# One-hot rows turned by ScalarE, value parts added in PSUM, and the sums of two layers kept by tokens

## The chip, the cores and the metric

The kernel runs on one core of a Trainium2 chip. The metric is the device time of one execution in microseconds (us), here the median of three runs. A profiled execution gives the trace that the rows below are from.

## What is computed

Two transformer blocks follow each other on 256 tokens of width 1024, all in float32. What the change touches is the second half of the first block, a layer that picks 16 experts per head out of 16384 (8 heads, so 128 picks per token), and the last layer of the second block:

```python
def peer(h, wq, subkeys, u, v):
    ...
    s1, i1 = lax.top_k(s[:, :, 0], P_TOPK)
    s2, i2 = lax.top_k(s[:, :, 1], P_TOPK)
    cand = (s1[..., :, None] + s2[..., None, :]).reshape(T, P_HEADS, P_TOPK * P_TOPK)
    sc, ci = lax.top_k(cand, P_TOPK)
    e = ...  # the first key's index * 128 + the second key's index
    g = jax.nn.softmax(sc, axis=-1)
    ...
        z = jnp.einsum('thkd,td->thk', jnp.take(u, eb, axis=0), hb)
        a = (jax.nn.gelu(z) * gb)
        return jnp.einsum('thk,thkd->td', a, jnp.take(v, eb, axis=0))

# first block:   x = x + g2 * rms_norm(peer(h), norm2_post)
# second block:  x = x + jnp.square(jax.nn.relu(h @ w_up)) @ w_down
```

## The kernel before, in words

Nothing is gathered. The kernel computes z for all 16384 experts and all tokens as dense products (128 chunks of 128 experts, `z_chunks`), applies gelu, multiplies each z by a weight that is zero for experts a token did not pick, and multiplies the result by the whole of v (128 chunks again, `out_chunks`). The order is: queries and routing beside z chunks 0 to 43, z chunks 44 to 95, output chunks 0 to 31, z chunks 96 to 127, output chunks 32 to 127. Four tiles `zt[0]` to `zt[3]` hold 32 chunks of z each.

Every product of two float32 matrices is made of three matmuls of type fp32r: each operand is split into a high part and a low part (`wh`, `wl`; `hh`, `hl`; `ah`, `al`), and high by high, low by high and high by low are added in PSUM (`mm3`, L184 to L186). For weights, `split` does this on the fly: a 1 MB block comes by DMA (`raw`), ScalarE (ACT) casts half of it to `wh` (L164), and VectorE (DVE) or GpSimd (POOL) subtracts to get `wl` (L165). Which engine subtracts is a set of half-block numbers given to `chunks` as `pool_`; for z's weights it was halves 0 to 49 and every second one up to 94. There are three buffers each of `raw`, `wh` and `wl` in this part of the program, so the weights are ready two to three chunks ahead at most. A z chunk and an output chunk are 24 matmuls each, of 128x128 weights and 256 columns. For the output, `acc_k` keeps the sums by features: the 128x128 blocks of v are loaded as weights, the 256 tokens are streamed.

The weight of an expert for a token comes from two one-hots. `weights_of(s, n)` treats n groups of 32 chunks at once, in three passes (group 0, groups 1 and 2, group 3), in blocks of TB = 16 tokens: `o1` (L1023) is, for every token, the one-hot of the first key's index, as a row of 128; `o2` (L1027) is the one-hot of the second index, with tokens innermost; `og` (L1031) is `o2` times the two parts (high, low) of the softmax value. One float16 matmul per token (L1038) has `o1`'s row block as weights and streams both parts of `og` side by side: 64 columns for n = 1, 128 for n = 2, and since tokens are innermost, one column lies 32 bytes from the next. ACT and DVE then add the two parts (L1041, L1042) and DVE multiplies z (L1046). `weights_of` is a generator: `advance(bg, n)` runs n of its steps (up to the next `yield`) after each chunk, with the rates NW, NX, NY, and `drain` runs what is left. The routing is a generator too (`bgr`, rate NR).

After the last output chunk the sums of squares go over the partitions by matmuls (`sums`, `norm`), the result is scaled and added to x (`residual`), and the parts of the next layer's input are made. The first half-blocks of the second block's first weights are split ahead, in places given by `LB`; the `wl` of all six are on POOL. In the last layer, `wup` and `wdn` chunks alternate; `acc_k` sums `wdn` by features as well.

Instructions stand on each engine's queue in one fixed order; what cannot start holds up all behind it on that queue.

Of the kernel before, what the change touches and what calls it, by code (L numbers as in the profile page):

```python
# [22 lines left out]
TB = 16  # L23
# [10 lines left out]
LB = ('qaee',(0,1,2,3,4,5))  # L34
KO = 3
F2 = (5,10)
KA = 0
KB = 2
PU = (4,50,1)
NZ, NR, NW, ZR, NX, NY = (7, 1.75, 1, 44, 0.8, 1)  # L40
# [71 lines left out]
def body(ctx: ExitStack, tc: tile.TileContext, a: dict):  # L112
# [125 lines left out]
    def acc_k(acc, *steps, first=False, last=False, order=range(8), then=lambda j: None):  # L238

        for j in order:  # L240
# [3 lines left out]
            then(j)  # L244

# [572 lines left out]
    with ExitStack() as p2:  # L818
# [197 lines left out]
        def weights_of(s, n):  # L1016


            m = 32 * n
            for b in range(S // TB):  # L1020
# [4 lines left out]
                yield  # L1025
# [3 lines left out]
                og = op_.tile([128, 2, 64, TB], F16, tag="og", name="og", bufs=2)[:, :, :m]  # L1029
# [455 lines left out]
```

## Time and profile before

| | |
|---|---|
| median of 3 runs | 1618.21 us (1616.15 to 1618.53) |
| the profiled execution | 1615.83 us |
| its span (first to last instruction) | 1614.0 us |
| TensorE (PE) matmuls busy | 1536.8 us, 95% of the span |
| VectorE (DVE) busy | 1235.1 us, 77% |
| ScalarE (ACT) busy | 762.0 us, 47% |
| GpSimd (POOL) busy | 243.6 us, 15% |
| mean granted TensorE clock | 0.972 of full speed |

The span is what the trace covers; 1.83 us of the profiled execution lie around it. Matmuls overlap each other in the pipeline, so "PE busy" says when PE had work, and not how fast it went: the pace is read from the starts of successive matmuls. The stages of the part that changes are: routing with z chunks (371 to 558 us in the trace), z with the first pass of weights (558 to 745), output and z with the second pass (745 to 970), the rest of the second pass alone (970 to 994), output with the third pass (994 to 1162), output alone (1162 to 1298), and the join to the second block (1298 to 1328). The last layer is at 1434 to 1614.

### The profile page before, as it was taken

The page shows a single profiled execution, that of the slowest core. Times are in us where ns is not written, and L with a number is a line of the kernel's source. Part 1 is how long each engine was busy: PE and PEld are TensorE (multiplying, and loading weights), DVE is VectorE, ACT ScalarE, POOL GpSimd, SP SyncE. Part 2 cuts the span into 40 slices and gives each one's busy share as a digit, 9 for nine tenths or more (in the row PEclk, how much of TensorE's full clock was granted, in tenths as well). Part 3 has the DMA queues.
Part 4 walks back from the last instruction along what each step waited for, and adds up shares of the span by engine and source line. Part 5 has one row for each costly group of instructions (what it writes and reads, how often), then busy time and mean ns, then how long its engine had stood idle before and what let it go on. Part 6 is the DMA issues. An engine that isn't in the chain of part 4 may idle for free.

```text
span 1614.0 us, 29532 instructions
## 1 busy us (share of the span) xinstructions
PE 1536.8 (95%) x12164; PEld 1475.0 (91%) x12164; DVE 1235.1 (77%) x2231; ACT 762.0 (47%) x1263; POOL 243.6 (15%) x109
## 2 busy tenths in 40 slices
PE   5899999989888999999999997999999989999998
PEld 4898899979888999999899985999999979899998
DVE  8978796677969999887877778888755578666555
ACT  3544454445435434444444443444444458754442
POOL 3300000034436843330000000000000030000000
PEclk7999999999999999999999997999999989999999
DMA  9456594534433534444434341444455535344542
GB/s 347 178 196 240 204 336 175 185 120 169 168 132 134 182 134 153 150 144 161 173 134 154 134 156 51 157 153 145 159 191 190 183 121 183 105 155 186 183 184 79
DMA packets 40025, 269.82 MB, mean 167 GB/s; under 512 B 4433, under 2 KB 5201, under 8 KB 9170
## 3 DMA queue, kind: packets, MB, share of 16 engines
q1 hardware_dynamic: 38882, 264.67, 45.5%
q10 hardware_dynamic: 1008, 3.27, 0.6%
q8 instruction: 95, 1.56, 0.4%
q14 instruction: 40, 0.33, 0.1%
HBM read 266.87 MB, written 1.05 MB: 166 GB/s over the span
## 4 chain that ended last, share of the span: by engine, by line
PE 83%; DVE 14%; ACT 2%; issue 1%; DMA 0%; SPq 0%; DVEq 0%; ACTq 0%
PE mm L184 12%; PE mm L186 12%; PE mm L185 12%; PE acc L185 10%; PE acc L186 10%; PE acc L184 10%; PE g L1038 7%; DVE wl L165 1%; DVE cand L877 1%; DVE scr L411 1%; DVE x L342 1%; DVE pr L917 1%; DVE o L1023 1%; PE mm L218 1%; DVE i L871 1%
## 5 line engine op out<-in xcount | busy, mean ns | idle before, releaser
L164 ACT CAST wh<-raw 128x1024 fp32r<-128x1024 f32 x449 | 470.0, 1049 | 623.6 <-PE mm L185 315.1
L165 DVE TENSOR_TENSOR wl<-raw,wh 128x1024 fp32r<-128x1024 f32 x361 | 441.8, 1229 | 175.8 <-ACT wh L164 173.1
L186 PE MATMUL mm<-hh,wl 128*128 128x256 f32 x1816 | 516.4, 284 | 12.3 <-DVE wl L165 12.0
L184 PE MATMUL mm<-hh,wh 128*128 128x256 f32 x1816 | 521.5, 287 | 4.4 <-ACT z L854 4.4
L185 PE MATMUL mm<-hl,wh 128*128 128x256 f32 x1816 | 513.4, 283 | 0.0
L186 PEld LDWEIGHTS mm<-hh,wl 128*128 128x128 f32 x1816 | 346.6, 191 | 15.0 <-DVE wl L165 13.7
L184 PEld LDWEIGHTS mm<-hh,wh 128*128 128x128 f32 x1816 | 345.9, 190 | 11.3 <-ACT z L854 4.6
L185 PEld LDWEIGHTS mm<-hl,wh 128*128 128x128 f32 x1816 | 346.6, 191 | 0.8 <-issue 0.2
L165 POOL TENSOR_TENSOR wl<-raw,wh 128x1024 fp32r<-128x1024 f32 x89 | 227.1, 2558 | 492.5 <-PE mm L312 252.8
L184 PE MATMUL acc<-ah,wh 128*128 128x256 f32 x1024 | 289.4, 283 | 2.0 <-ACT ah L248 2.0
L185 PE MATMUL acc<-al,wh 128*128 128x256 f32 x1024 | 288.6, 282 | 0.0
L186 PE MATMUL acc<-ah,wl 128*128 128x256 f32 x1024 | 288.4, 282 | 0.0
L184 PEld LDWEIGHTS acc<-ah,wh 128*128 128x128 f32 x1024 | 194.6, 190 | 3.9 <-ACT ah L248 2.5
L185 PEld LDWEIGHTS acc<-al,wh 128*128 128x128 f32 x1024 | 193.9, 189 | 0.3
L186 PEld LDWEIGHTS acc<-ah,wl 128*128 128x128 f32 x1024 | 193.3, 189 | 0.0
L1023 DVE TENSOR_TENSOR o<-row,idxT 128x2048 f16<-128x2048 f16 x48 | 123.7, 2577 | 66.1 <-PE g L1038 66.1
L1038 PE MATMUL g<-og,o 128*128 128x64 f16 (+1 forms) x768 | 129.9, 334 | 12.2 <-DVE u L1042 6.5
L1038 PEld LDWEIGHTS <-o 128*128 128x128 f16 x768 | 83.0, 115 | 38.9 <-issue 8.1
L1138 POOL MEMSET q<- 128x2048 f32 x1 | 1.8, 1809 | 557.7 <-DVE al L249 557.7
L185 PE MATMUL acc<-ml,wh 128*128 128x256 f32 x256 | 72.3, 283 | 0.0
L186 PE MATMUL acc<-mh,wl 128*128 128x256 f32 x256 | 72.2, 282 | 0.0
L184 PE MATMUL acc<-mh,wh 128*128 128x256 f32 x256 | 71.9, 282 | 0.0
(435 smaller groups left out, 2194.9 us busy)
## 6 DMA issues: line engine op xcount, KB each, us to landing
raw<-in_uT_dram SPq DMA_DIRECT2D x64, 1024.0 KB, 4.8
raw<-in_ev_dram SPq DMA_DIRECT2D x64, 1024.0 KB, 4.8
araw<-in_wada_dram SPq DMA_DIRECT2D x16, 1024.0 KB, 5.8
raw<-in_wup_dram SPq DMA_DIRECT2D x16, 1024.0 KB, 4.7
raw<-in_wdn_dram SPq DMA_DIRECT2D x16, 1024.0 KB, 4.8
raw<-in_wcxb_dram SPq DMA_DIRECT2D x12, 1024.0 KB, 4.8
araw<-in_wada_dram SPq DMA_DIRECT2D x16, 512.0 KB, 9.9
raw<-in_wout_dram SPq DMA_DIRECT2D x8, 1024.0 KB, 4.8
```

The source lines that it names most:

```text
L164: by.copy(wh, raw) if by is A else by.tensor_copy(wh, raw)
L165: on.tensor_sub(wl, raw, wh)
L184: T.matmul(ps, lhsT=wh, rhs=xh, start=start, stop=False, skip_group_check=skip)
L185: T.matmul(ps[:, :n], lhsT=wh, rhs=xl, start=False, stop=False, skip_group_check=skip)
L186: return T.matmul(ps, lhsT=wl, rhs=xh, start=False, stop=stop, skip_group_check=skip)
L218: T.matmul(ps, lhsT=w, rhs=xh[:, k, :n], start=k == 0, stop=False)
L342: V.tensor_add(x[:, j, :], x[:, j, :], u)
L411: return V.scalar_tensor_tensor(out=scr, in0=raw, scalar=0.5, in1=crow, op0=ALU.mult, op1=ALU.mult, accum_out=ada[:, j:j + 1])
L871: V.max_index(out=ti[:, i, 8:16], in_max=tv[:, i, 8:16], in_values=rep)
L877: V.tensor_add(cand[:, :, o:o + n], tv2[:, :, 0, ra:ra + 1].to_broadcast([128, 2, n]), tv2[:, :, 1, 0:n])
L1023: V.tensor_tensor(out=o1, in0=row16[:, None, :].to_broadcast([128, TB, 128]), in1=idxT[:, 0, ts_, None].to_broadcast([128, TB, 128]), op=A ...
L1038: T.matmul(ps[:, t], lhsT=o1[:, k * nt + t, :], rhs=og[:, :, :, k * nt + t], start=True, stop=True)
```

## The change

In `weights_of`, blocks are of 8 tokens. `os`, the one-hot of the first index, is made with tokens innermost, and ACT copies it to `o1` with the token outermost. `ow` is `o2` times both value parts in one instruction, and ACT copies it to `og`, where one part's 32 or 64 columns of a token lie next to each other. Two matmuls per token (L1063 of the changed kernel), one for each part, add into the same PSUM columns, and one DVE instruction per group scales the sum and multiplies z. The next block is made before the matmuls of the present one. The rates are NW = 1.25 and NX = NY = 1.05.

The output sums and those of `wdn` are kept by tokens (`acc_tok`): the 128 tokens of `ah`, `al` (or `mh`, `ml`) are the weights, 512 columns of `wh` or `wl` are streamed, 12 matmuls for a chunk. The norm after the experts' layer is then a sum along the free dimension (`ended`), and 16 transposes bring its result back to features. At the end x is transposed to tokens by 16 transposes beside the last layer (`turn`), and the result leaves by tokens.

POOL makes `wl` for the even ones of z's half-blocks 0 to 48, 25 in all, and none for the second block's first weights.

```diff
-TB = 16
+TB = 8
-LB = ('qaee',(0,1,2,3,4,5))
+LB = ('', ())
-NZ, NR, NW, ZR, NX, NY = (7, 1.75, 1, 44, 0.8, 1)
+NZ, NR, NW, ZR, NX, NY = (7, 1.75, 1.25, 44, 1.05, 1.05)
+    def acc_tok(acc, *steps, first=False, last=False, then=lambda t, c: None):
+        for t in range(2):
+            ts_ = slice(t * 128, (t + 1) * 128)
+            for c in range(2):
+                cs = slice(c * 512, (c + 1) * 512)
+                for n, ((wh, wl), (xh, xl)) in enumerate(steps):
+                    T.matmul(acc[t][c], lhsT=xh[:, ts_], rhs=wh[:, cs], start=first and n == 0, stop=False)
+                    T.matmul(acc[t][c], lhsT=xl[:, ts_], rhs=wh[:, cs], start=False, stop=False)
+                    T.matmul(acc[t][c], lhsT=xh[:, ts_], rhs=wl[:, cs], start=False, stop=last and n == len(steps) - 1)
+                then(t, c)
...
-                o1 = op_.tile([128, TB, 128], F16, tag="o1", name="o1", bufs=2)
-                V.tensor_tensor(out=o1, in0=row16[:, None, :].to_broadcast([128, TB, 128]),
-                                in1=idxT[:, 0, ts_, None].to_broadcast([128, TB, 128]), op=ALU.is_equal)
+                os = op_.tile([128, 128, TB], F16, tag="os", name="os", bufs=1)
+                V.tensor_tensor(out=os, in0=io16, in1=idxT[:, 0, None, ts_].to_broadcast([128, 128, TB]),
+                                op=ALU.is_equal)
+                o1 = op_.tile([128, TB, 128], F16, tag="o1", name="o1", bufs=2)
+                A.copy(o1, os.rearrange("p n t -> p t n"))
...
-                for i in range(2):
-                    V.tensor_tensor(out=og[:, i], in0=o2, in1=gT[:, i, None, ts_].to_broadcast([128, m, TB]),
-                                    op=ALU.mult)
+                V.tensor_tensor(out=ow, in0=o2[:, None].to_broadcast([128, 2, m, TB]),
+                                in1=gT[:, :, None, ts_].to_broadcast([128, 2, m, TB]), op=ALU.mult)
+                A.copy(og, ow.rearrange("p i n t -> p t i n"))
...
-                        T.matmul(ps[:, t], lhsT=o1[:, k * nt + t, :], rhs=og[:, :, :, k * nt + t], start=True, stop=True)
-                    A.activation(u, ps[:, :, 0].rearrange("p t n -> p n t"), AF.Copy, scale=1.0 / GS)
-                    V.scalar_tensor_tensor(out=u, in0=ps[:, :, 1].rearrange("p t n -> p n t"), scalar=1.0 / GS, in1=u,
-                                           op0=ALU.mult, op1=ALU.add)
-                        V.tensor_mul(zz, zz, u[:, 32 * q_:32 * q_ + 32])
+                for t in range(TB):
+                    for i in range(2):
+                        T.matmul(ps[:, t], lhsT=o1[:, t, :], rhs=og[:, t, i], start=i == 0, stop=i == 1)
+                for q_ in range(n):
+                    zz = zt[s + q_][:, :, b * TB:(b + 1) * TB]
+                    V.scalar_tensor_tensor(out=zz, in0=ps[:, :, 32 * q_:32 * q_ + 32].rearrange("p t n -> p n t"),
+                                           scalar=1.0 / GS, in1=zz, op0=ALU.mult, op1=ALU.mult)
-        cu = chunks(a["uT"], range(64), pool_={*range(50), *range(50, 96, 2)})
+        cu = chunks(a["uT"], range(64), pool_={*range(0, 50, 2)})
...
+        def ended(t, c):
+            A.activation(yt[:, t, c * 512:(c + 1) * 512], acc[t][c], AF.Square, accum_out=rt[:, t, c:c + 1])
+            if c == 0:
+                return
+            V.tensor_add(rt[:, t, 2:3], rt[:, t, 0:1], rt[:, t, 1:2])
+            A.activation(rt[:, t, 3:4], rt[:, t, 2:3], AF.Sqrt, bias=epsc, scale=1.0 / D)
+            V.reciprocal(rt[:, t, 4:5], rt[:, t, 3:4])
+            A.activation(yt[:, t, 0:512], acc[t][0], AF.Copy, scale=rt[:, t, 4:5])
+            V.tensor_scalar(out=yt[:, t, 512:1024], in0=acc[t][1], scalar1=rt[:, t, 4:5], scalar2=None, op0=ALU.mult)
...
-        residual(m2, x, acc, ry, prm[:, 24:32], lambda j: scaled(x, KS("n12"), hh3, hl3, j))
+                V.scalar_tensor_tensor(out=x[:, j, ts_], in0=turned[t][j // 4][:, j % 4 * 128:j % 4 * 128 + 128],
+                                       scalar=prm[:, 24 + j:25 + j], in1=x[:, j, ts_], op0=ALU.mult, op1=ALU.add)
+                if t == 1:
+                    scaled(x, KS("n12"), hh3, hl3, j)
```

Three places show how the order on the engines moves. The names in the rows are those of the tiles (`o` with a number is a buffer of `o1` or `o2`), out of the arrow's left side, in on its right. On PE, in the second pass beside the output chunks, before:

```order
L1038 LDWEIGHTS o_8470
L1038 MATMUL g<-og,o_8470 128x128
L1038 LDWEIGHTS o_8470
L1038 MATMUL g<-og,o_8470 128x128
L184 MATMUL acc<-ah,wh 128x256
L185 MATMUL acc<-al,wh 128x256
L186 MATMUL acc<-ah,wl 128x256
```

and now:

```order
L1063 LDWEIGHTS o_8827
L1063 MATMUL g<-og,o_8827 128x64
L1063 LDWEIGHTS o_8827
L1063 MATMUL g<-og,o_8827 128x64
L253 MATMUL acc<-wh,ah 128x512
L254 MATMUL acc<-wh,al 128x512
L255 MATMUL acc<-wl,ah 128x512
```

Each token's matmul of 128 columns became two of 64 columns with the same weights loaded twice, and the output matmuls stream twice as many columns, half as many of them. Before, the last 56 matmuls of this pass stood in a row behind the last z chunk, with nothing between; now the last 16 stand ahead of the last three z chunks. The second place is DVE in the same stretch, before:

```order
L1023 TENSOR_TENSOR o_9318<-row_6289,idxT 128x2048
L1042 SCALAR_TENSOR_TENSOR u<-g,u 128x256 x2
L1046 TENSOR_TENSOR z<-z,u 128x32x4 x4
L165 TENSOR_TENSOR wl<-raw,wh 128x1024
L249 TENSOR_TENSOR al<-z,ah 128x256
L165 TENSOR_TENSOR wl<-raw,wh 128x1024
L249 TENSOR_TENSOR al<-z,ah 128x256
L165 TENSOR_TENSOR wl<-raw,wh 128x1024
L249 TENSOR_TENSOR al<-z,ah 128x256
L1031 TENSOR_TENSOR og<-o_9352,gT 128x1024 x2
L1027 TENSOR_TENSOR o_9565<-io_3918,idxT 128x1024
```

and now, one block of 8 tokens with its two output chunks:

```order
L1037 TENSOR_TENSOR os<-io_3918,idxT 128x1024
L1045 TENSOR_TENSOR ow<-o_9336,gT 128x1024
L261 TENSOR_TENSOR al<-z,ah 128x256
L1042 TENSOR_TENSOR o_9407<-io_3918,idxT 128x512
L164 TENSOR_TENSOR wl<-raw,wh 128x1024
L261 TENSOR_TENSOR al<-z,ah 128x256
L1066 SCALAR_TENSOR_TENSOR z<-g,z 128x32x8 x2
L164 TENSOR_TENSOR wl<-raw,wh 128x1024
```

The wide comparison with a broadcast index is gone, the sum of the parts is gone, and a block now goes with two output chunks. The third place is DVE in the routing, where sums over 16 steps (`pr`) are made, before:

```order
L928 TENSOR_TENSOR pr<-m,pick 128x1024
L955 RECIPROCAL sm<-sm 128x8
L917 TENSOR_TENSOR pr<-pr 128x512
L959 TENSOR_TENSOR gp<-ex,sm 128x4x16
L917 TENSOR_TENSOR pr<-pr 128x256
L959 TENSOR_TENSOR gp<-ex,sm 128x4x16
L917 TENSOR_TENSOR pr<-pr 128x128
```

and now:

```order
L940 TENSOR_TENSOR pr<-m,pick 128x1024
L967 RECIPROCAL sm<-sm 128x8
L164 TENSOR_TENSOR wl<-raw,wh 128x1024
L929 TENSOR_TENSOR pr<-pr 128x512
L971 TENSOR_TENSOR gp<-ex,sm 128x4x16
L929 TENSOR_TENSOR pr<-pr 128x256
L971 TENSOR_TENSOR gp<-ex,sm 128x4x16
```

A `wl` of z's weights now stands among the routing's instructions, and the z chunk that it belongs to waits for it; before, all of these were on POOL's queue here.

## Rows read from the trace of the kernel before

**Rows 1.** The page: busy time of the engines, and the chain that ended last.

```profile
PE 1536.8 (95%) x12164; PEld 1475.0 (91%) x12164; DVE 1235.1 (77%) x2231; ACT 762.0 (47%) x1263; POOL 243.6 (15%) x109
...
PE 83%; DVE 14%; ACT 2%; issue 1%; DMA 0%; SPq 0%; DVEq 0%; ACTq 0%
```

**Rows 2.** By stage: stretch, length, busy PE, weight loads, DVE, ACT, POOL; clock; DMA.

```profile
371.00:558.00 187.00, 170.30 (x1375) 167.89 (x1373) 159.76 (x576) 86.64 (x131) 107.54 (x44) 0.96 0.43 153
558.00:745.00 187.00, 183.80 (x1533) 182.87 (x1532) 168.00 (x173) 82.19 (x143) 72.17 (x27) 0.98 0.43 151
745.00:970.00 225.00, 225.00 (x1709) 203.26 (x1708) 169.78 (x289) 100.40 (x173) 0.00 (x0) 1.00 0.42 150
970.00:994.00 24.00, 13.43 (x54) 6.26 (x52) 20.76 (x51) 7.32 (x18) 0.00 (x0) 0.60 0.05 19
...
1162.00:1297.00 135.00, 135.00 (x1148) 135.00 (x1147) 73.66 (x98) 62.94 (x96) 1.81 (x1) 1.00 0.52 186
1297.00:1328.00 31.00, 23.31 (x158) 21.79 (x157) 23.47 (x37) 15.60 (x36) 14.68 (x6) 0.78 0.36 123
```

**Rows 3.** Pieces of the chain: start, time in the chain, what; 64 and 128 columns.

```profile
581.71 1.89 PE g L1038 x16
...
757.26 1.86 PE g L1038 x8
```

**Rows 4.** Groups of weight loads, whole run: weights, count, busy, mean ns of one.

```profile
L184 PEld LDWEIGHTS acc<-ah,wh 128*128 128x128 f32 x1024 | 194.6, 190 | 3.9 <-ACT ah L248 2.5
...
L1038 PEld LDWEIGHTS <-o 128*128 128x128 f16 x768 | 83.0, 115 | 38.9 <-issue 8.1 <-DVE og L1031 6.2
...
L1302 PEld LDWEIGHTS o<-zs,v 128*64 128x64 f32 x16 | 2.2, 137 | 1.3
```

**Rows 5.** PE's timeline, float32 matmuls (two instructions each): start, us, columns.

```profile
1298.64 1.03 PE L294 MATMUL mm<-ones,sq 128*128 128x1 f32 x8
1299.53 1.36 PE L302 MATMUL g<-ones 128*128 128x128 f32 x10
...
1401.09 0.60 PE L1293 MATMUL mm<-e,cc 128*128 128x256 f32 x2
1401.52 0.38 PE L1294 MATMUL mm<-e,ones 128*128 128x128 f32 x2
```

**Rows 6.** Groups of DVE and ACT at 745 to 970 us, POOL idle.

```profile
L165 DVE TENSOR_TENSOR wl<-raw,wh 128x1024 fp32r<-128x1024 f32 x63 | 76.3, 1220 | 25.1 <-ACT wh L164 25.1
...
L164 ACT CAST wh<-raw 128x1024 fp32r<-128x1024 f32 x64 | 67.1, 1049 | 115.0 <-PE mm L185 48.8 <-PE acc L185 37.1 <-issue 27.3
...
L1042 DVE SCALAR_TENSOR_TENSOR u<-g,u 128x256 f32<-128x256 f32 x50 | 19.2, 416 | 1.5 <-ACT u L1041 1.5
...
L1031 DVE TENSOR_TENSOR og<-o,gT 128x1024 f16<-128x1024 f16 x24 | 15.4, 683 | 0.0
L854 ACT ACTIVATE z<-mm 128x256 f32<-128x256 f32 x31 | 11.7, 377 | 0.0
```

**Rows 7.** The same multiplication with 512 elements, at 994 to 1162 us.

```profile
L1031 DVE TENSOR_TENSOR og<-o,gT 128x512 f16<-128x512 f16 x32 | 13.2, 415 | 0.0
```

**Rows 8.** DVE's timeline in the routing: POOL idle in the first, busy in the second.

```profile
423.43 0.42 DVE L917 TENSOR_TENSOR pr<-pr 128x512 f16<-128x512 f16 x1
...
437.31 3.19 DVE L917 TENSOR_TENSOR pr<-pr 128x512 f16<-128x512 f16 x3
```

**Rows 9.** Waits at 371 to 558 us: total, times, longest.

```profile
PE mm L186 <- DVE wl L165: 12.0, 5, 5.8
```

**Rows 10.** Busy time where the first pass of weights begins.

```profile
558.00:572.00 14.00, 10.80 (x88) 10.58 (x87) 13.53 (x11) 4.93 (x9) 11.53 (x4) 0.88 0.42 152
```

**Rows 11.** The timeline at the join to the second block.

```profile
1299.88 7.18 POOL L165 TENSOR_TENSOR wl<-raw,wh 128x1024 fp32r<-128x1024 f32 x3 [8.64 <-ACT wh L164]
...
1302.57 4.76 DVE L342 TENSOR_TENSOR x<-x,u 128x256 f32<-128x256 f32 x2
...
1305.44 0.92 PE L218 MATMUL mm<-hh,wh 128*128 128x256 f32 x4 [1.86 <-ACT hh L321]
```

More of the change, by code (lines that the diff above doesn't have):

```diff
@@ new lines, in made_of @@
+                A.copy(og, ow.rearrange("p i n t -> p t i n"))
+                return o1, og
+            blocks = S // TB
+            next_ = made_of(0)
+            yield
+            for b in range(blocks):
+                o1, og = next_
+                if b + 1 < blocks:
+                    next_ = made_of(b + 1)
+                    yield
+                ps = gt()[:, :TB * m].rearrange("p (t n) -> p t n", t=TB)
+                for t in range(TB):
[5 more added lines that the diff above has]
+                                           scalar=1.0 / GS, in1=zz, op0=ALU.mult, op1=ALU.mult)
+                yield
@@ L1070, in out_chunks @@
                     continue
-                acc_k(acc, *steps, first=i == 0, last=i == 127)
+                acc_tok(acc, *steps, first=i == 0, last=i == 127, then=ended if i == 127 else lambda t, c: None)
                 steps.clear()
@@ L1100, in body @@
         drain(bg)
+        yt = zq[1].tile([128, 32, 256], F32, tag="z1", name="yt")[:, :8].rearrange("p (t j) n -> p t (j n)", t=2)
         out_chunks(96, 128)
-        ssy = mmt(258)
         raws = [load(a["wqk2"][b]) for b in range(2)]
-        total = presum(m2, acc, 6)
-        last, mm = sums(m2, ssy, acc, total, 6)
-        add = added[0]
-        ry, _, root, inv, end = norm(m2, ssy, gt(), mm, F2)
-        places = dict(q=(A, last), r=(A, root), e=(A, end), a=(V, add), i=(V, inv), n=(A, None))
-        hh3, hl3 = halves()
-        residual(m2, x, acc, ry, prm[:, 24:32], lambda j: scaled(x, KS("n12"), hh3, hl3, j))
+        hh3, hl3 = halves()
+        turned = [[gt() for _ in range(2)],
+                  [pacc.tile([128, 512], F32, tag=f"acc{i}", name="turned") for i in range(2)]]
+        for t in range(2):
+            ts_ = slice(t * 128, (t + 1) * 128)
+            for j in range(8):
+                T.transpose(turned[t][j // 4][:, j % 4 * 128:j % 4 * 128 + 128], yt[:, t, j * 128:(j + 1) * 128],
+                            C("ident"))
+            if t == 0:
+                fill(mmt(), F2)
+            for j in range(8):
+                V.scalar_tensor_tensor(out=x[:, j, ts_], in0=turned[t][j // 4][:, j % 4 * 128:j % 4 * 128 + 128],
+                                       scalar=prm[:, 24 + j:25 + j], in1=x[:, j, ts_], op0=ALU.mult, op1=ALU.add)
+                if t == 1:
+                    scaled(x, KS("n12"), hh3, hl3, j)
     with ExitStack() as p3:
@@ L1146, in body @@
         rows = psl.tile([104, 256], F32, name="rows")
-        cqk = chunks(a["wqk2"], range(4), raws, {i: places[t] for i, t in enumerate(LB[0])}, LB[1])
+        cqk = chunks(a["wqk2"], range(4), raws, {}, LB[1])
         pss, ws = [mmt(), mmt(), pz.tile([128, 384], F32, tag="o", name="mm3", bufs=1)[:, :256],
@@ L1329, in body, with turn @@
             scaled(x, KS("n22"), hh, hl, j)
-        acc = Banks(pacc)
+        acc = [[pacc.tile([128, 512], F32, tag=f"acc{2 * t + c}", name="acc") for c in range(2)] for t in range(2)]
+        xt = zs8.rearrange("p h c t -> p (h c t)")[:, :2048].rearrange("p (t n) -> p t n", t=2)
+        def turn(i):
+            t, q = divmod(i, 4)
+            pt = pz.tile([128, 384], F32, tag=("o", "zr")[i % 2], name="pt", bufs=1)
+            for k in range(2):
+                T.transpose(pt[:, k * 128:(k + 1) * 128], x[:, 2 * q + k, t * 128:(t + 1) * 128], C("ident"))
+            A.copy(xt[:, t, q * 256:(q + 1) * 256], pt[:, :256])
         cu, cd = chunks(a["wup"], range(16)), chunks(a["wdn"], range(16))
@@ L1352, in body @@
                 k = min(n - 1, 29)
-                acc_k(acc, (next(cd), mid[k]), first=k == 0)
+                acc_tok(acc, (next(cd), mid[k]), first=k == 0)
             if n == 4:
@@ L1482 @@
     r = _run(nc, [arrays], core_ids=[0])
[L1483 to L1484 removed]
+    o = r.results[0]["out_0_dram"].reshape(128, 2, 1024)
+    return np.ascontiguousarray(o.transpose(1, 0, 2)).reshape(1, 256, 1024)
```

59 lines of the change are left out of this document (22 added, 37 removed).

## The prediction

> **What bounds the kernel now.** I read the page first: matmuls are busy 95% of the span and the chain that ended last is 83% PE, 14% DVE [rows 1]. So PE's queue is nearly all of the time, and a change pays if it shortens what PE runs or fills a stage in which PE waits. The view by stage tells which is which [rows 2]. In three stages PE is busy all the time at full clock (745 to 970, 1162 to 1297, and nearly so 558 to 745); there only the length of PE's own work counts. At 970 to 994 PE is busy 13.43 of 24.00 us at a clock of 0.60, and at the join, 1297 to 1328, 23.31 of 31.00 at 0.78: there PE waits. In the routing stage, 371 to 558, PE lacks 16.7 us of 187, while DVE is busy 159.76.
>
> PE's pace comes from counts, since matmuls overlap: 1148 of 256 columns in 135 us are 117.6 ns each, 0.46 ns a column, 2.82 us for a chunk of 24 [rows 2]. The one-hot matmuls are in the pieces of the chain: 16 of 64 columns in 1.89 us (118 ns), 8 of 128 columns in 1.86 us (232 ns) [rows 3]. Half the columns, half the time: these are held by streaming, at 1.8 ns a column, four times what contiguous columns cost.
>
> **The change, part by part.**
>
> *One-hot matmuls.* Before: two passes of 16 groups at 1.89 us and one of 32 at 1.86, so 60.5 + 59.5 = 120 us, in stages where PE is full. After: two per token and pass, 256 x 3 x 2 = 1536, each with a weight load, 1024 of 32 columns and 512 of 64, contiguous. No row has such a pair. Weight loads of float32 take 190 ns for 128 columns and 137 for 64 [rows 4], so 0.83 ns a column above a fixed 84; the float16 load of 128 columns takes 115, that is 31 above the fixed part. Streaming at 0.46 ns a column is 15 ns for 32 and 29 for 64. Load and stream one after the other: 46 and 60 ns, 1024 x 0.046 + 512 x 0.060 = 78 us, **minus 42**. Bounds: if the stream hides under the load, 31 ns each, 48 us (minus 72). The shortest pace that a row shows for any row of pairs is that of one-column float32 matmuls, 8 in 0.89 us, 111 ns [rows 5]; then 170 us, plus 50. I take the value near the lower end, because the 111 ns are explained by the float32 load (128 x 0.83 = 106), which a float16 one does not have.
>
> [...]
>
> *Sums by tokens.* 128 chunks of v and 32 of `wdn` go from 24 x 117.6 ns to 12 matmuls of 512 columns. If time goes with columns, that is 12 x 235 ns and nothing is won. The lower end: a float32 instruction of 256 columns, which passes at half rate and so keeps PE as long as 512 columns here would, takes 0.43 / 2 = 215 ns [rows 5]: 2.58 us a chunk, minus 39 for 160 chunks. I take the middle, 225 ns (half of the excess over that row is per column, half per matmul): 0.12 us a chunk, **minus 20**.
>
> *The end of the second pass.* 56 matmuls stood behind the last z chunk; they are 7 groups of 1.86 us, 13 of the 24 us at 970 to 994 [rows 2, 3]. The other 11 are waits of PE, ACT and DVE for each other. The new generator has 64 steps and gets 64 x 1.05 = 67 in this stage, and the order has its last group three chunks before the end: **minus 11** (bounds 0 and minus 11).
>
> *Start of the first pass.* PE idles 3.2 of 14 us, at a clock of 0.88 [rows 10], where the first `og` is late. Now a block is made ahead and DVE's part of it is shorter: **minus 3** (0 to minus 5).
>
> *The join.* The 31 us [rows 2] hold 96 matmuls of the next product, 11.3 us; the rest is a chain over partitions and a DVE that POOL holds up: two additions of 256 elements take 4.76 us while POOL subtracts, and the first product matmul starts at 1305.44 [rows 11]. After: ACT runs square, cast, root, cast, copy behind the last matmul, about 0.6 + 1.05 + 0.3 + 1.05 + 0.6 = 3.6 us (512 elements interpolated from 377 and 1049 ns [rows 6]); then DVE has one `wl`, 8 additions of 128 elements (about 0.28) and 8 low parts (0.42), 6.8 us; then 32 low matmuls, 3.8. With 4 us for a low clock and the transposes, some 20 us: **minus 10** (minus 4 to minus 14).
>
> *The last layer.* 16 transposes of 128 columns at about 0.11 us on PE: **plus 2**.
>
> *What DVE and ACT must hide.* In the second pass a block of 8 tokens goes with two output chunks: PE 2 x 2.70 + 16 x 0.060 = 6.4 us. DVE: two chunks at 73.66 / 47.8 = 1.54 us [rows 2], `os` and `ow` at 0.683, `o2` at 0.415, two scalings at 0.416 [rows 6, 7], together 5.7 us, 89%. ACT: two chunks at 62.94 / 47.8 = 1.32, two copies of 1024 elements at 1.05 if they run like the cast [rows 6], 4.7 us. In the first and third pass both have more room. I price the coupling of queues this full at **plus 5** (0 to 15).
>
> *POOL's part.* In the routing POOL ran 44 subtractions, now about 22; DVE gets the other 22, 22 x 1.22 = 27 us [rows 2, 6]. But a DVE instruction of these sums takes 0.42 us when POOL is idle and three of them 3.19 us when it is not [rows 8], so each subtraction that POOL does costs DVE up to 1.9 us; 22 fewer give back some 20 to 40. DVE's load stays about what it is. What is new: z chunks wait for a `wl` that stands behind routing work, where until now PE waited for DVE 12 us in all [rows 9]. I take **0**, with 15 to either side.
>
> Sum: -42 -20 -11 -3 -10 +2 +5 +0 = -79. The profiled execution took 1615.83 us, so 1537; the median of the runs lies 2.4 above it, so **1540 us**.
>
> **Rivals.**
>
> *Pairs at the pace of one-column matmuls (the slower side).* If a weight load and a matmul, however small, can't follow the last pair in less than the 111 ns of [rows 5], the 1536 take 170 us and the time is 1540 + 92 = 1632 us. For it: no stretch of this trace runs pairs faster. Against it: the float32 loads explain that pace. It decides from 1540 - 1618 = -78, so at (78 + 78) / 1536, about 102 ns a pair.
>
> [...]
>
> *ACT's copies read with a step.* The copies to `o1` and `og` read every eighth float16, 16 bytes apart. PE read 32 bytes apart at 1.8 ns a column [rows 3]; if ACT reads so, 1024 elements take about 1.8 + 0.16 = 2.0 us. Second pass: 32 x (1.05 + 0.38) + 32 x 1.32 + 64 x 2.0 = 216 us of ACT, against 32 x 2.82 + 32 x 2.70 + 31 = 207 of PE; the two other passes come level with PE. ACT would set the pace, at plus 25 with the coupling: 1565 us. For it: the step. Against it: none of the kernel's ACT rows reads SBUF so; ACT may have the rate to spare.
>
> [...]
>
> *DVE late in the routing.* If the locked instructions don't give back what the 22 subtractions cost, DVE's 159.76 us become some 185 in a stage of 187 in which it also waits for scores, and PE waits with it: plus 25, 1565 us.
>
> **How the numbers follow.** My sum holds with a chance of 0.58, within 1492 (pairs at 31 ns, 512 columns at 215) and 1565; pairs at about 80 ns 0.12; pairs at 111 ns 0.11; ACT's copies 0.10; DVE in the routing 0.09. The range 1492 to 1600 leaves out the pairs at 111 ns and a little at the ends. Within 0.2%, about what a measurement of this kernel can tell from no change, lies only a pair price near 102 ns, 0.03; slower is what is left of the 111 ns case, 0.10; faster 0.87.
>
> **What would show it.** The one-hot groups in the chain: 16 in about 0.74 us (32 columns) and 0.96 (64) if right, 1.8 if the first rival holds. Output matmuls: 12 in 2.70 us a chunk. ACT's copy of 1024 elements: 1.05 us, or near 2. No stretch between the last z chunk and output chunk 32. At the join 20 us from last output matmul to the end of the product, DVE's additions at 0.3. In the routing DVE's sums mostly at 0.4, and PE's waits for `wl` not far over 12 us. The prediction is wrong if the pair costs over 75 ns, or if DVE or ACT, and not PE, ends the passes.

## The result, and the profile after

The changed kernel takes 1528.67 us (1527.6 to 1530.23, 4 runs), the kernel before 1618.35 on the same chips: a ratio of 0.945, 95% interval 0.9433 to 0.9466, so 86 to 92 us less. I had forecast 1540, with 1492 to 1600 as the range. The profiled execution took 1527.6 us, its span is 1525.8; before they were 1615.83 and 1614.0. The spans differ by 88.2 us, and that is what the parts below must add up to. The line of the page that answers to [rows 1]:

```profile
PE 1458.6 (96%) x11020; PEld 1324.9 (87%) x11020; DVE 1117.2 (73%) x2185; ACT 1020.7 (67%) x1338; POOL 104.2 (7%) x55
```

PE, DVE and POOL are busy less; ACT's time went from 762 to 1020.7 us. The view by stage says where that is (columns as in [rows 2]): z chunks with the first pass of weights, output and z chunks with the second, output with the third, output alone, the join.

```profile
558.00:728.00 170.00, 165.52 (x1766) 163.46 (x1764) 121.29 (x188) 163.74 (x172) 4.81 (x2) 1.00 0.48 162
728.00:938.00 210.00, 203.28 (x1665) 178.04 (x1666) 163.36 (x265) 207.37 (x199) 0.00 (x0) 1.00 0.47 161
938.00:1132.00 194.00, 194.00 (x1280) 154.01 (x1280) 147.07 (x245) 173.90 (x189) 0.00 (x0) 1.00 0.51 174
1132.00:1222.00 90.00, 90.00 (x393) 72.81 (x392) 51.15 (x67) 46.68 (x71) 1.81 (x1) 1.00 0.58 198
1222.00:1238.00 16.00, 14.23 (x118) 13.61 (x117) 15.19 (x39) 12.91 (x29) 0.00 (x0) 1.00 0.46 160
```

In the first two stages the fullest engine is ACT, 163.74 of 170 and 207.37 of 210 us, and PE has gaps. In the third PE is the bound again. The join runs at full clock, where [rows 2] had 0.78. ACT's time is explained by three groups of the page (instruction, shapes, count, busy and mean ns of one, idle time ahead of them):

```profile
L163 ACT CAST wh<-raw 128x1024 fp32r<-128x1024 f32 x450 | 471.8, 1051 | 376.5 <-PE mm L184 216.7
...
L1040 ACT COPY o<-os 128x1024 f16<-128x1024 f16 x96 | 197.4, 2056 | 3.1 <-DVE os L1037 3.1
L1049 ACT COPY og<-ow 128x512 f16<-128x512 f16 (+1 forms) x96 | 137.4, 1432 | 0.0
```

The cast of 1024 contiguous elements takes 1051 ns as before; the copy of 1024 float16 that are read with a step takes 2056. That rival's price held. The pace of PE is read from the starts in its timeline (start, us, what), in the second pass and in the third:

```profile
804.28 0.64 PE L1063 MATMUL g<-og,o 128*128 128x64 f16 x16
804.76 0.48 PE L253 MATMUL acc<-wh,ah 128*128 128x512 f32 x1
...
1049.94 0.56 PE L1063 MATMUL g<-og,o 128*128 128x32 f16 x16
1050.35 0.48 PE L253 MATMUL acc<-wh,ah 128*128 128x512 f32 x1
1050.67 0.39 PE L254 MATMUL acc<-wh,al 128*128 128x512 f32 x1
1050.90 0.40 PE L255 MATMUL acc<-wl,ah 128*128 128x512 f32 x1
1051.14 0.39 PE L253 MATMUL acc<-wh,ah 128*128 128x512 f32 x1
1051.37 0.39 PE L254 MATMUL acc<-wh,al 128*128 128x512 f32 x1
```

From the start of a group of 16 one-hot matmuls to the start of the next matmul it takes 0.48 us with 64 columns and 0.41 with 32; [rows 3] had 1.89 for 16 matmuls of 64 columns and 1.86 for 8 of 128. Inside a group one matmul starts 25 ns after the last with 32 columns and 29 ns with 64, weight load included. Matmuls of 512 columns start 0.23 us apart: 1051.37 less 1050.67 is 0.70 for three. In the stretch of output alone they are 232 ns apart on average, and before 256 columns were 118: by the column nearly the same.

PE's waits in the routing, the answer to [rows 9] (total, times, longest):

```profile
PE mm L185 <- DVE wl L164: 15.2, 9, 3.0
PE mm L185 <- POOL wl L164: 1.2, 2, 1.1
```

One of these waits in the timeline of the three engines:

```profile
489.34 2.40 POOL L164 TENSOR_TENSOR wl<-raw,wh 128x1024 fp32r<-128x1024 f32 x1 [3.30 <-ACT wh L163]
489.55 3.27 DVE L164 TENSOR_TENSOR wl<-raw,wh 128x1024 fp32r<-128x1024 f32 x1
492.87 0.39 PE L185 MATMUL mm<-hh,wl 128*128 128x256 f32 x1 [1.49 <-DVE wl L164]
```

DVE's subtraction starts 0.21 us after POOL's and lasts until 492.82, which is 1.08 us after POOL's end, instead of 1.22 in all; PE stands for 1.49 us. Nine waits make up the 15.2 us. In three of them POOL holds the `wl` itself, as here; in three others it holds an instruction that stands ahead of the `wl` on DVE's queue, and these six are 12 us of the 15. The fourth of the nine, where PE stands for 1.83 us; the first of DVE's instructions took 0.42 us in [rows 8] when POOL was idle:

```profile
432.62 2.40 POOL L164 TENSOR_TENSOR wl<-raw,wh 128x1024 fp32r<-128x1024 f32 x1 [18.25 <-ACT wh L163]
...
432.79 2.51 DVE L929 TENSOR_TENSOR pr<-pr 128x512 f16<-128x512 f16 x1
435.22 1.21 DVE L164 TENSOR_TENSOR wl<-raw,wh 128x1024 fp32r<-128x1024 f32 x1
```

The cast of this `wl`'s `wh` had ended at 429.69; the `wl` began 5.5 us later, as the instruction ahead of it on DVE's queue ended.

The same named matmuls bound the stages in every run, so their lengths can be set side by side. Each is the difference between the starts of two matmuls, but that the join begins with the end of the last output matmul. The join ends with the first matmul of the second block's first output product, which an expectation below calls the first `wdn` matmul; so it holds the second block's first layers, which are the same in both, and the last column holds that product, 49 us, besides `wup` and `wdn`. The runs below are described in the next section.

| us | z 0 to 43 and routing | z 44 to 95, pass 1 | out 0 to 31, z 96 to 127, pass 2 | out 32 to 95, pass 3 | out 96 to 127 | join | last layer |
|---|---|---|---|---|---|---|---|
| before | 150.7 | 184.5 | 253.3 | 213.1 | 90.6 | 90.2 | 221.3 |
| after | 153.2 | 170.0 | 209.6 | 194.4 | 89.3 | 79.3 | 221.1 |
| one matmul a token | 154.3 | 169.9 | 209.4 | 188.0 | 89.3 | 79.3 | 221.1 |
| copies read in a row | 153.2 | 164.5 | 198.3 | 194.4 | 89.3 | 79.3 | 221.1 |
| rows by DVE | 153.3 | 167.2 | 198.4 | 194.4 | 89.3 | 79.3 | 221.0 |
| old POOL set | 153.6 | 171.5 | 209.6 | 194.4 | 89.3 | 79.3 | 220.9 |
| none on POOL | 132.9 | 169.2 | 211.1 | 194.4 | 89.3 | 79.3 | 221.0 |
| old weights | 153.8 | 184.3 | 251.9 | 211.2 | 89.3 | 82.0 | 221.0 |
| rows by DVE, none on POOL | 132.9 | 165.5 | 198.4 | 194.4 | 89.3 | 79.3 | 221.0 |

### The profile page after: what moved, and what is told of

It is laid out like the page before. It is cut to its first block, busy times and chain, and to the rows that moved or that the text cites. A ratio compares the mean times of both kernels' runs of the same rounds, so it can differ in the third digit from the quotient of the medians.

```text
span 1525.8 us, 27313 instructions
## 1 busy us (share of the span) xinstructions
PE 1458.6 (96%) x11020; PEld 1324.9 (87%) x11020; DVE 1117.2 (73%) x2185; ACT 1020.7 (67%) x1338; POOL 104.2 (7%) x55
## 3 DMA queue, kind: packets, MB, share of 16 engines
HBM read 266.61 MB, written 1.05 MB: 175 GB/s over the span
## 5 line engine op out<-in xcount | busy, mean ns | idle before, releaser
L163 ACT CAST wh<-raw 128x1024 fp32r<-128x1024 f32 x450 | 471.8, 1051 | 376.5 <-PE mm L184 216.7
L164 DVE TENSOR_TENSOR wl<-raw,wh 128x1024 fp32r<-128x1024 f32 x415 | 511.7, 1235 | 191.1 <-ACT wh L163 186.4
L185 PE MATMUL mm<-hh,wl 128*128 128x256 f32 x1816 | 515.3, 284 | 16.5 <-DVE wl L164 15.2
L253 PE MATMUL acc<-wh,ah 128*128 128x512 f32 x512 | 205.9, 402 | 1.8 <-ACT wh L163 1.0
L255 PE MATMUL acc<-wl,ah 128*128 128x512 f32 x512 | 202.5, 395 | 0.7 <-DVE wl L164 0.5
L254 PE MATMUL acc<-wh,al 128*128 128x512 f32 x512 | 202.0, 395 | 0.9 <-DVE al L261 0.9
L1040 ACT COPY o<-os 128x1024 f16<-128x1024 f16 x96 | 197.4, 2056 | 3.1 <-DVE os L1037 3.1
L1049 ACT COPY og<-ow 128x512 f16<-128x512 f16 (+1 forms) x96 | 137.4, 1432 | 0.0
L255 PEld LDWEIGHTS acc<-wl,ah 128*128 128x128 f32 x512 | 96.2, 188 | 26.7 <-DVE wl L164 4.6
L164 POOL TENSOR_TENSOR wl<-raw,wh 128x1024 fp32r<-128x1024 f32 x35 | 87.7, 2510 | 450.4 <-PE mm L324 252.9
L253 PEld LDWEIGHTS acc<-wh,ah 128*128 128x128 f32 x512 | 96.2, 188 | 22.7 <-ACT wh L163 1.4
L254 PEld LDWEIGHTS acc<-wh,al 128*128 128x128 f32 x512 | 96.1, 188 | 21.6 <-DVE al L261 1.2
L1063 PEld LDWEIGHTS <-o 128*128 128x128 f16 x1536 | 46.5, 96 | 16.9 <-issue 13.7
L1063 PE MATMUL g<-og,o 128*128 128x32 f16 (+1 forms) x1536 | 56.6, 182 | 1.5 <-ACT og L1049 1.5
```

The source lines that it names most:

```text
L163: by.copy(wh, raw) if by is A else by.tensor_copy(wh, raw)
L164: on.tensor_sub(wl, raw, wh)
L185: return T.matmul(ps, lhsT=wl, rhs=xh, start=False, stop=stop, skip_group_check=skip)
L253: T.matmul(acc[t][c], lhsT=xh[:, ts_], rhs=wh[:, cs], start=first and n == 0, stop=False)
L254: T.matmul(acc[t][c], lhsT=xl[:, ts_], rhs=wh[:, cs], start=False, stop=False)
L255: T.matmul(acc[t][c], lhsT=xh[:, ts_], rhs=wl[:, cs], start=False, stop=last and n == len(steps) - 1)
```

## The experiments

**Output matmuls of 256 columns.** In `acc_tok`:

```diff
-                    T.matmul(acc[t][c], lhsT=xh[:, ts_], rhs=wh[:, cs], ...)
+                    for e in range(2):
+                        to = acc[t][c][:, e * 256:e * 256 + 256]
+                        cs = slice(c * 512 + e * 256, c * 512 + e * 256 + 256)
+                        T.matmul(to, lhsT=xh[:, ts_], rhs=wh[:, cs], ...)
...
```

> The changed kernel with each 512-column matmul of the output sums and of wdn made as two of 256 columns (24 a chunk again). Theory A, from the trace of after: a 512-column matmul starts 233 ns after the last and a 256-column one 118 ns, so time goes with columns and 160 chunks lose 24 x 118 - 12 x 233 = 36 ns each, 6 us at most: 1530 to 1535 us. Rival, my prediction's term: a matmul has a fixed part and the wide ones won 20 us: 1547 to 1550 us.

Measured: 1540.11 us (1539.01 to 1543.73), 11 more than the changed kernel, between the two. In the stretch of output alone each of these matmuls starts 120 ns after the last, against 118 by features before and 116 per 256 columns in the wide form, and the weight loads leave no gap:

```profile
1150.00:1230.00 80.00, 80.00 (x669) 80.00 (x668) 44.23 (x56) 38.44 (x57) 1.81 (x1) 1.00 0.52 184
```

So the width is worth 2 ns or so per 256 columns against the kernel before, as theory A has it for that comparison, and 4 against this form. Why 256 columns by tokens are slower than by features stays open.

**One matmul per token.** The low part of the softmax values is left out.

```diff
-                    for i in range(2):
-                        T.matmul(ps[:, t], lhsT=o1[:, t, :], rhs=og[:, t, i], start=i == 0, stop=i == 1)
+                    T.matmul(ps[:, t], lhsT=o1[:, t, :], rhs=og[:, t, 0], start=True, stop=True)
```

> The changed kernel with one matmul per token, the one with the high part of og (the low parts are left out): 768 fewer pairs of weight load and matmul, 512 of 32 and 256 of 64 columns. Theory A: a pair costs PE the 25 and 29 ns between the starts of matmuls in the trace, and ACT, busy 98% of the first two passes, sets their pace; only the third pass gives anything back, 256 x 25 ns = 6 us: 1521 to 1525 us. Rival 1: PE sets the pace of all three passes: 768 pairs give 20 us, 1507 to 1511 us. Rival 2: a pair costs the 46 to 60 ns of the prediction and PE sets the pace: 39 us, 1490 us.

Measured: 1522.04 us (1520.37 to 1522.38), 6.6 less, as theory A has it. The table shows it: the third pass is 6.4 us shorter, 25 ns for each of 256 pairs, and the other two gave back nothing. The pair costs 25 ns, and where ACT is the bound it costs nothing.

**ACT's copies read in a row.** The sizes stay, but nothing is turned, so the one-hots are not those of the tokens.

```diff
-                A.copy(o1, os.rearrange("p n t -> p t n"))
+                A.copy(o1, os.rearrange("p n t -> p (n t)").rearrange("p (t n) -> p t n", t=TB))
-                A.copy(og, ow.rearrange("p i n t -> p t i n"))
+                A.copy(og, ow.rearrange("p i n t -> p i (n t)").rearrange("p i (t n) -> p t i n", t=TB))
```

> The changed kernel with both of ACT's copies reading contiguously (same sizes, but the rows are not turned, so the one-hots are wrong). Theory A: the step of 16 bytes makes the copy of 1024 elements take 2.06 us; read contiguously it takes 1.05 or less, ACT's busy time in the first two passes falls by some 100 us of 373, and the waits there go: PE's own work in the two passes is 52 x 2.82 + 13 and 64 x 2.81 + 15, 159 and 195 us, against 170 and 210, so 15 to 25 us off: 1504 to 1514 us. Rival: the waits there have another cause (DVE's order, the weights' casts behind the copies whatever these take): within 4 us of 1529. Rival on the step: the copy of float16 takes 2 us in any order: 1529 us and an ACT row still near 2.0.

Measured: 1511.48 us (1511.23 to 1511.88), 17.2 less: theory A. The group of the copy, and the view by stage over the first two passes (columns as above):

```profile
L1040 ACT COPY o<-os 128x1024 f16<-128x1024 f16 x96 | 99.8, 1040 | 3.1 <-DVE os L1037 3.1
```

```profile
559.00:723.00 164.00, 163.93 (x1760) 162.39 (x1759) 124.53 (x192) 118.77 (x175) 4.81 (x2) 1.00 0.50 168
723.00:921.00 198.00, 198.00 (x1664) 177.22 (x1664) 163.16 (x262) 146.73 (x195) 0.00 (x0) 1.00 0.50 171
```

The step alone made the copy twice as long, 2056 against 1040 ns. Without it ACT has room and PE no gap. All of the 17 us come from these two passes (5.5 and 11.3).

**Rows made by DVE.** `os` and its copy go; DVE makes `o1` directly, as it did before.

```diff
-                V.tensor_tensor(out=os, in0=io16, in1=idxT[:, 0, None, ts_].to_broadcast([128, 128, TB]), op=ALU.is_equal)
...
-                A.copy(o1, os.rearrange("p n t -> p t n"))
+                V.tensor_tensor(out=o1, in0=row16[:, None, :].to_broadcast([128, TB, 128]),
+                                in1=idxT[:, 0, ts_, None].to_broadcast([128, TB, 128]), op=ALU.is_equal)
...
+        row16 = op_.tile([128, 128], F16, name="row16")
+        V.tensor_copy(row16, io16[:, :, 0])
```

> The changed kernel with o1 made as rows by DVE in one comparison with a broadcast index, as before, and no os and no copy of it; og still goes over ACT. DVE's comparison took 2.29 us for 2048 elements, so 1.15 for 1024 against 0.69 of os: DVE gets 96 x 0.46 = 44 us more over the three passes, ACT 96 x 2.06 = 197 us less. Theory A: ACT's copies bind the first two passes, so 15 to 25 us off, 1504 to 1514 us, with ACT near 65% of them and DVE under 90%. Rival: DVE becomes what ends the waits in the second pass (162 + 15 of 195 us and a chain to ACT and back): no gain there, 1519 to 1529 us.

Measured: 1515.09 us (1514.05 to 1515.55), 13.6 less, a little short of theory A. The second pass gets all of it back (198.4 us), the first half of it. The group of the comparison, and the second pass by stage:

```profile
L1037 DVE TENSOR_TENSOR o<-row,idxT 128x1024 f16<-128x1024 f16 x96 | 116.8, 1216 | 0.0
```

```profile
726.00:924.00 198.00, 197.96 (x1661) 177.20 (x1662) 176.83 (x263) 147.15 (x163) 0.00 (x0) 1.00 0.50 170
```

DVE at 89% of the second pass does not hold PE up. Why the first pass gets back only half stays open.

**Columns 16 bytes apart.** No copy to `og`; the two matmuls stream `ow` (two buffers of it), which goes by the name `og` at the matmul.

```diff
-                A.copy(og, ow.rearrange("p i n t -> p t i n"))
-                return o1, og
+                return o1, ow
...
-                        T.matmul(ps[:, t], lhsT=o1[:, t, :], rhs=og[:, t, i], start=i == 0, stop=i == 1)
+                        T.matmul(ps[:, t], lhsT=o1[:, t, :], rhs=og[:, i, :, t], start=i == 0, stop=i == 1)
```

> The changed kernel without ACT's copy to og: the two matmuls of a token stream ow directly, tokens innermost, so one column lies 16 bytes from the next. Theory A: what made the old one-hot matmuls slow is the step between columns, and 16 bytes cost as much as 32 did, 1.8 ns a column: groups of 16 start 58 ns (32 columns) and 115 ns (64) apart, 118 us instead of 40 for the three passes, and ACT's 137 us of copies go, which gives back some 10 us of waits in the first two passes: 1590 to 1600 us. Rival 1: the cost goes with the step, half of it at 16 bytes (0.9 ns a column, 29 and 58 ns): plus 19, minus 10: 1533 to 1540 us. Rival 2: the step costs the matmuls nothing and one pair per part was the gain: 1510 to 1520 us.

Measured: 1587.17 us (1586.42 to 1588.66), 58.5 more than the changed kernel; theory A, a little under its range. Matmuls of 32 columns start 60 ns apart and those of 64 columns 116, 1.8 to 1.9 ns a column. In PE's timeline, first pass and second:

```profile
602.54 1.12 PE L1060 MATMUL g<-ow,o 128*128 128x32 f16 x16
...
830.10 2.02 PE L1060 MATMUL g<-ow,o 128*128 128x64 f16 x16
```

By these paces the matmuls cost 1024 x 35 + 512 x 87 ns = 80 us more; the time rose by 58.5, so some 22 came back with ACT's copies. So a step of 16 bytes was as slow here as one of 32 (1.8 to 1.9 ns a column against 1.8), and the gain of the one-hot part is the contiguous columns, not that there are two matmuls.

**The old set of GpSimd's half-blocks, and none.** In the changed kernel:

```diff
-        cu = chunks(a["uT"], range(64), pool_={*range(0, 50, 2)})
+        cu = chunks(a["uT"], range(64), pool_={*range(50), *range(50, 96, 2)})
```

and, for none, `pool_=()`.

> The changed kernel with the old set of half-blocks whose wl GpSimd makes (0 to 49 and every second one up to 94, 73 instead of 25). Theory A, from the traces: POOL's share hardly matters, since what it takes off DVE in the routing (some 22 subtractions, 27 us) it gives back by slowing DVE's two-byte instructions; PE waited there 10.6 us for wl before and 15.4 after, so at most 5 us faster: 1524 to 1529 us. Rival 1: fewer subtractions on POOL were a gain of their own, by the locks that they spared DVE: 1535 us or more. Rival 2: DVE's load decides and not the locks: 22 x 1.22 = 27 us less on DVE, the routing's waits for wl go: 1513 to 1517 us.

> The changed kernel with all of z's low parts on DVE and none on GpSimd. Theory A: share hardly matters in this direction either, DVE gets 25 x 1.22 = 30 us and loses what POOL's remaining 44 us in the routing cost it: within 5 us of 1529. Rival 1 (DVE's load decides): plus 15 to 25. Rival 2 (the locks decide): minus 5 to 12.

Measured: 1532.6 us (1530.9 to 1533.43) with the old set, 3.9 more; 1504.57 us (1503.73 to 1505.04) with `pool_=()`, 24.1 less. My theory fell for the second: rival 2 holds, and by more than it asked for. Time against the number of subtractions on POOL is 73: 1532.6, 25: 1528.7, 0: 1504.6. The run with the old set is nearest to theory A, with the sign of rival 1. The routing's stage (z chunks 0 to 43) by busy time in the changed kernel, then without POOL, and then PE's wait for `wl` there without it:

```profile
405.00:558.00 153.00, 137.13 (x1092) 134.52 (x1092) 121.01 (x458) 66.46 (x99) 44.26 (x18) 0.97 0.44 150
```

```profile
401.00:534.00 133.00, 131.90 (x1094) 130.03 (x1092) 118.86 (x474) 66.60 (x99) 0.00 (x0) 1.00 0.50 173
```

```profile
PE mm L185 <- DVE wl L164: 0.4, 2, 0.2
```

DVE is not busier, though it makes 44 `wl` in this stage and not 26: each takes it 1216 ns, where 3 of the 26 were held and took 2.0 to 3.3 us, and its other instructions are no longer held either. Of the 20 us by which the stage is shorter, some 15 are PE's idle time (15.9 us against 1.1) and 5 its busy time, at a granted clock of 0.97 and 1.00. The other 4 us lie ahead of the first z chunk.

**The join without POOL, in the kernel before.**

```diff
-LB = ('qaee',(0,1,2,3,4,5))
+LB = ('', ())
```

> The kernel before with one line changed: the first half-blocks of the second block's first weights are split in the ordinary way, none of their low parts on POOL. It isolates POOL's part of the join, which the changed kernel shortened by 11 us in all (from the end of the last output matmul to the first wdn matmul, 90.2 to 79.3). Theory A: the gain at the join is the shorter chain (sums along the free dimension, transposes), and POOL's six subtractions mattered little: DVE gets 6 x 1.22 = 7 us more in the same place and is rid of the locks: within 3 us of the kernel before. Rival: POOL held DVE up, and half or more of the 11 us came from that line alone: 5 us or more faster than before.

Measured: 1610.25 us (1609.19 to 1613.13), ratio 0.9962 (0.9951 to 0.9974), so 4 to 8 us less: the rival. Between the matmuls of the table its join is 83.4 us, against 90.2 before. The two additions that took 4.76 us in [rows 11]:

```profile
1306.26 0.75 DVE L342 TENSOR_TENSOR x<-x,u 128x256 f32<-128x256 f32 x2
```

**The changed set alone, and none, in the kernel before.** The line of `cu` as above, in the kernel before.

> The kernel before with one line changed: GpSimd makes wl of every second half-block from 0 to 48 (25 in place of 73), the part of the change that I priced at 0 with 15 to either side. Theory A, from the last runs: fewer subtractions help only where none is left, since one on GpSimd holds DVE for as long as it runs and the wl that a z chunk waits for is now on DVE, behind it; the routing comes out level, within 5 us of the kernel before. Rival 1: this line alone gives a good part of the change's 90 us, 10 us or more faster. Rival 2: DVE needs the help beside the one-hots, which in this kernel it makes alone: 10 us or more slower.

> The kernel before with no low part of z's weights on GpSimd. Theory A (GpSimd's subtractions stop DVE, whatever else the kernel does): the routing's waits go as they did in the changed kernel, minus 15 to 22 us, and beside the first pass of one-hots DVE gets 26 x 1.22 = 32 us and is rid of slow instructions (16 blocks with 0.76 + 0.80 + 2 x 0.55 us each = 43 us), so nothing is lost there: 1593 to 1603 us. Rival: in this kernel DVE is too full beside the one-hots and takes it back: within 5 us of the kernel before, or slower.

Measured: the changed set 1612.28 us (1612.07 to 1613.78), ratio 0.9969 (0.9958 to 0.998), 3 to 7 us less, theory A's 5 or a little over; none 1589.89 us (1587.92 to 1590.79), ratio 0.9827, 28 us less, more than theory A asked for. Of these, 17.7 lie in the routing's stage, 5.4 in the first pass and 4.1 ahead of the first z chunk. With no subtraction on POOL, DVE makes the rows of 16 tokens in 2292 ns each beside the first pass, where the kernel before took 3053 (its line first).

```profile
L1023 DVE TENSOR_TENSOR o<-row,idxT 128x2048 f16<-128x2048 f16 x18 | 54.9, 3053 | 16.0 <-PE g L1038 16.0
...
L1023 DVE TENSOR_TENSOR o<-row,idxT 128x2048 f16<-128x2048 f16 x16 | 36.7, 2292 | 28.3 <-PE g L1038 28.3
```

**Both edits that helped.** Rows by DVE and `pool_=()` in the changed kernel.

> The changed kernel with both of the edits that made it faster: o1 made as rows by DVE (minus 13.6 us alone) and no low part of z's weights on GpSimd (minus 24 alone). Theory A: the two act in different stages (the routing; the first two passes) and add up: 1491 us, with 3 to either side. Rival: DVE, which gets 44 us of comparisons and 30 of subtractions, is then what PE waits for in the passes, and part is lost: 1496 to 1505 us.

Measured: 1487.84 us (1487.53 to 1488.76), ratio 0.9198 to the kernel before (0.9185 to 0.921), 40.8 us below the changed kernel: the two add up, and 3 us more. The line of the page:

```profile
PE 1446.5 (97%) x11020; PEld 1317.8 (89%) x11020; DVE 1155.5 (78%) x2211; ACT 847.9 (57%) x1242; POOL 42.0 (3%) x30
```

**The change without its one-hot part.** The old `weights_of` (TB = 16, its rates, the old POOL set) in the changed kernel:

```diff
-TB = 8
+TB = 16
-NZ, NR, NW, ZR, NX, NY = (7, 1.75, 1.25, 44, 1.05, 1.05)
+NZ, NR, NW, ZR, NX, NY = (7, 1.75, 1, 44, 0.8, 1)
...
-                    for i in range(2):
-                        T.matmul(ps[:, t], lhsT=o1[:, t, :], rhs=og[:, t, i], start=i == 0, stop=i == 1)
+                        T.matmul(ps[:, t], lhsT=o1[:, k * nt + t, :], rhs=og[:, :, :, k * nt + t], start=True, stop=True)
...
```

> The changed kernel with the old weights_of (blocks of 16 tokens, one matmul per token over both parts, no copies by ACT), its rates and the old set of GpSimd's half-blocks: what is left of the change is the sums by tokens, the join by tokens and without POOL, and the turning of x. Theory A, from the traces: 512 columns cost what 2 x 256 do less some 2 ns, so 128 output chunks give 5 us and the last layer nothing; the join gives 11: 1618.4 - 16 = 1602 us, 1599 to 1605. Rival, my prediction's term: the wide matmuls give 20 us and the join 10: 1586 to 1590 us.

Measured: 1604.7 us (1603.47 to 1606.18), ratio 0.992 (0.9906 to 0.9933), 11 to 15 us less than before: theory A. By the table the three stretches with output chunks are 1.4, 1.9 and 1.3 us shorter, 4.6 for the sums by tokens, the last layer 0.3, the join 8.2. So the one-hot part, with its rates and its POOL set, is worth 76 us of the 90. No run changes the block size, the making ahead or the rates by themselves.

The join is 2.7 us longer here than in the changed kernel, though the lines of the join are the same. Ten matmuls of ones by ones, whose result nothing reads (`fill` in the kernel), run at 1222 us in the join of the changed kernel; in this run they ran at 973 us, in a wait of the second pass. At the join PE then idles 2.89 us ahead of the second half of the transposes, where it idled 0.66, and the clock of the first 16 us is 0.79, where the line above of the changed kernel has 1.00:

```profile
1297.00:1313.00 16.00, 12.00 (x75) 11.27 (x74) 13.86 (x37) 10.55 (x24) 0.00 (x0) 0.79 0.48 157
```

## Why the prediction came out as it did

The direction and the range were right, and the time was 11 us too high. But two terms were off by some 15 us and one by 38, and they nearly cancelled: that 1540 came within 11 us is in good part luck. Before to after, by the prediction's own terms (the three passes' own work is counted from the paces, the waits are what is left of a stage's length):

| term, us | predicted | measured |
|---|---|---|
| one-hot matmuls | -42 | -79.6 |
| sums by tokens | -20 | -4.6 |
| waits of the passes: start, drain, coupling (-3 -11 +5) | -9 | +5.9 |
| join | -10 | -10.9 |
| turning x (with the last layer's sums) | +2 | -0.2 |
| POOL in the routing | 0 | +2.5 |
| the rest: ahead of the first z chunk, the end | | -1.3 |
| sum | -79 | -88.2 |

**One-hot matmuls: right in mechanism, mis-sized.** The step that failed is "load and stream one after the other: 46 and 60 ns", and the bound of 31 ns too. I took the float16 load's 115 ns in [rows 4], subtracted the fixed part of the float32 loads and added the stream. The pair costs 25 and 29 ns: 1024 x 25 + 512 x 29 = 40 us against 120. The load's own duration, 96 ns on average in the trace, is hidden behind the pairs ahead of it, which start 25 and 29 ns apart. That the 1.8 ns a column of [rows 3] were the price of the step between columns was shown by the run that brought a step back, and the price by the run that took half of the pairs away.

**Sums by tokens: the step that failed** is "half of the excess over that row is per column, half per matmul". The float32 row that gave 215 ns is another kind of matmul: its 256 columns took 215 ns where those of fp32r took 117.6 [rows 2, 5], 1.83 times as long, and not twice as the forecast had it. 512 columns took 232, so nearly all of it goes with columns. The run without the one-hot part gives 4.6 us where I had 20.

**The passes: the rival on ACT's copies was half right.** Its price was exact (2.0 us forecast, 2056 ns measured), its effect was not the 25 us that it gave: 17, by the run that reads in a row. My sum had the copies at 1.05. With them in a row the waits of the passes come to 5.9 - 16.8 = -11, near the -9 of the forecast, so the steps on the start and the drain hold: the 11 us of waiting behind the last z chunk went, and ACT's queue brought as much back inside the passes. Which part of the new order ended that waiting was not separated. By the sign that I had named, the prediction is wrong where "DVE or ACT, and not PE, ends the passes": ACT did in two of the three, so there the forecast had the wrong engine as the bound. The time stayed low all the same because the pairs cost half of what I had.

**The join: right.** From the last output matmul's end to the end of the next product it takes 18 us, 20 predicted (its parts add up to 18.2), 29 before. The prediction named both POOL and the old chain and did not say what each was worth: the one line that takes POOL out gives 4 to 8 of the 11 us even in the old chain, and what is left for the new one is some 4 us. The place of the ten matmuls of ones goes with 2.7 us, by one run that moved them unasked; no run moves them alone. The additions are 0.28 us each, as forecast:

```profile
1226.39 1.13 DVE L1148 SCALAR_TENSOR_TENSOR x<-turned,prm,x 128x128 f32<-128x128 f32 x4
...
1235.46 3.97 PE L222 MATMUL mm<-hh,wl 128*128 128x256 f32 x32
```

**POOL in the routing: 0 was right for this set and hid the larger thing.** The stage is 2.5 us longer. DVE's load did not stay what it was but fell, from 134.3 to 121.0 us: it got 18 more subtractions in this stage, 22 us, and was given back some 35, near the upper end of the 20 to 40 forecast. What I had not followed is what the subtractions that stay on POOL still hold: in six of PE's nine waits it was the `wl` for which PE waited next, or an instruction ahead of it on DVE's queue. With the old set PE waits nearly as long, 13.3 us, but in two waits, for the `wl` of other weights that stand behind the routing's instructions. So half the subtractions on POOL cost nearly as much as all of them, and none of them gives 20 us back in the routing. How long a subtraction on POOL holds one of DVE's instructions is in the rows at 432 and 489 us: these end 0.28 and 1.08 us behind POOL's and take 2.51 and 3.27 us, where they take 0.42 and 1.22 alone. The "locked" instructions of the prediction and the "locks" of the expectations are these; what holds them no run shows.

**The slower rival** (pairs at 111 ns) fell with 25 ns. The 0.12 for "pairs at about 80 ns" was given to a pace that no run shows; the runs showed 25 and 29. DVE late in the routing did not come: DVE's sums that took 0.42 us alone take 0.60 on average, and PE's waits for DVE's `wl` are 15.2 us in place of 12.

## What to carry to other kernels

Price a new pattern of small matmuls by their starts, not by the durations of their loads: here loads of 96 ns overlapped the pairs ahead, which started 25 and 29 ns apart, and a step between streamed columns made these matmuls two to four times as long (60 against 25 ns, 116 against 29). Work that moves to an idle engine takes its access pattern along: the step that was taken from TensorE came back on ScalarE, at twice the time of a plain copy (2056 against 1040 ns), and set the pace of two stages. Before splitting work between VectorE and GpSimd, try none on GpSimd: here every set tried with some of z's weights on it was slower, by up to 28 us.

## What was not expected of the hardware

A float16 weight load of 128 columns and a matmul of 32 or 64 columns follow the last pair in 25 and 29 ns, though a load takes 96 ns on average in the trace. A copy of 1024 float16 on ScalarE takes 2056 ns when read with a step of 16 bytes and 1040 in a row. Beside subtractions on GpSimd, VectorE's instructions with two tensor inputs were held and its searches were not: in the routing's stage of the kernel before, 28 of the first kind (TENSOR_TENSOR) began while one ran, more than 0.3 us ahead of its end, and 27 of them ended 0.03 to 1.08 us behind it (the other began within 0.01 us of its start and took 0.29), while 63 searches of one tensor (MAX8, FIND_INDEX8, MATCH_REPLACE8) kept their 0.2 to 0.3 us. Matmuls of 256 columns by tokens start 120 ns apart, 2 ns more than by features; that stays open.
